# Two plain gate-and-up sets: 128 tokens stationary and 512 weight columns streaming, instead of 128 weight columns stationary and 256 tokens streaming

## The chip, the cores and the metric

One core of a Trainium2 chip. The time is device microseconds of one execution. TensorE multiplies; a matmul has a stationary operand of 128 x 128 (loaded by its own instruction, shown as PEld) and a moving operand whose columns stream past it; results gather in eight PSUM banks of 128 x 512 floats. VectorE, ScalarE and GpSimd work beside it, and SyncE issues most of the DMA transfers.

## The reference

One decoder layer on 512 tokens, model width 2048: a mixer (attention and gated delta rule, merged), and then the dense channel mixer, which is what the change touches:

```
h = rmsnorm(x, norm_ffn) * (1 + sc_f) + sh_f            # 512 x 2048
gate, up = split(h @ w_gate_up)                         # 2 x (512 x 5632)
x = x + gt_f * ((silu(gate) * up) @ w_down)             # 512 x 2048
return rmsnorm(x, final_norm)
```

## The kernel before

All matrix products are made in three parts: each operand is split into a high part (`hi`, a ScalarE cast) and a low part (`lo`, a VectorE subtraction), and hi*hi, hi*lo and lo*hi are summed in PSUM. Activations are held transposed, features on the partitions. The 512 tokens are two halves h of 256.

`h2T[h][q]` is the split, normalised input of the channel mixer for half h and two k blocks (k = 2q, 2q+1) of 128 features; `h2_gen(h)` (line 1743) makes it: sums of squares by eight small matmuls (`hss`, in `part_rstd`), the reciprocal root on VectorE and a diagonal (`diag`), one product with ones that spreads it over the partitions (`hbc`, in `spread`), and then for each q two VectorE operations, two of ScalarE and the split (`h2h`, `h2l`).

The 5632 gate and up columns are done in 12 sets. Set 0 and set 1 are plain, of 256 gate and 256 up columns each; the ten big sets, `big(1)` to `big(10)`, of 512 + 512 columns, use seven products in place of eight on operands that are combined ahead: `combine()` (line 1769) makes `comb[q]` in four groups, each of four sums and four splits.

Set 0 (`gu0`, built with the helper `fm_set`) is done for half 0 and then for half 1, because the second half of `h2T` is not ready at its start; both fetch all the weights. Set 1 (`gu_both(1)`) does both halves together. In both a block of 128 weight columns is stationary and 256 tokens stream; the result has columns on the partitions, four banks of (128 columns x 2 halves of 256 tokens). `gu_done` takes the silu of the two gate banks (ScalarE), multiplies by the up banks (VectorE) and writes the two tiles to `f_dram[s, h]`, which the down stage reads, features on the partitions.

A big set has tokens stationary and 512 weight columns streaming, so its results come out with tokens on the partitions. They are turned one big set later: `turned_a(b)` (line 1938), called in four of the units of each big set's second half (`if second and 1 <= k <= 4`), makes four 128 x 128 transposes on TensorE into a bank `aT`; ScalarE copies it to `f`, and GpSimd writes it to `f_dram`. It does nothing while the list `turning` is empty, as it is in `big(1)`.

The order of work. `Driver` runs a list of units. A unit is a weight load, a split, and a list of matmuls; loads run up to four units ahead and splits two; before a unit's matmuls its `pre` is called, and then the next split is put out, or only after the matmuls where the unit is `late`. Beside the units run side chains, generators such as `h2_gen` and `combine`. Each 12 matmuls (`GROUP`) the driver pumps: each chain makes one step, and a chain that yields n lets n pumps pass. `hold()` holds one pump back. Where a unit needs what a chain has not made, its `pre` steps the chain on at once: in `gu0`, `ahead` demands `h2n[h] >= min(2 * i + 4, 16)` k blocks before unit i; in `big`, `pre(i)` demands `xn[0] > i % 8 // 2` groups of `comb`. TensorE, SyncE and GpSimd keep the order in which the program puts instructions out; ScalarE's and VectorE's order is chosen when the kernel is built. Tiles of 128 x 512 come from 68 shared slots (`S`), and a new tile waits for a free one. All matmuls and DMA issues show line 155, so the profile is read by tile names.

## Time and profile before

| | us |
|---|---|
| runs, median of 3 | 2736.91 (2732.53 to 2739.21) |
| profiled execution, first to last instruction (the span) | 2731.7 |
| profiled execution, own time | not recorded apart from the span |
| TensorE busy | 2705.7 |
| set 0 (tile gu, from 1379.7) and set 1 | together to 1473.35 |
| first big set | 1473.35 to about 1549 |

The profile is of one execution. PE is TensorE's matmuls, PEld its weight loads, DVE VectorE, ACT ScalarE, POOL GpSimd. A row of a timeline has the start, the length, the engine, the line, the operation, output and inputs, and in brackets the idle time before it and who ended it. The chain that ended last is followed back from the last instruction; its rows have start, length, engine, tile and the number of instructions. Rows of stretches give busy time of PE, PEld, DVE, ACT and POOL with instruction counts, the granted clock of TensorE as a fraction, the share of the DMA engines and GB/s. Matmuls overlap, so their cost is the distance from start to start, not their length.

### The profile page before, as it was taken

The numbers are of one execution on the slowest core, as the hardware profiler recorded it, in microseconds if no ns is written. First come the engines' busy times: TensorE is split into PE (matmuls) and PEld (weight loads), VectorE is DVE, ScalarE is ACT, GpSimd is POOL, SyncE is SP. The second block draws the span as 40 slices with busy tenths as digits, with TensorE's granted clock in tenths as the row PEclk, the third lists the DMA queues.
The fourth block names the chain that finished last, engine by engine and source line by source line (L and its number), as shares of the span: only waits on it lengthen the run. The fifth ranks groups of instructions, "written<-read, shape, count | busy, mean of one in ns | idle before, by whom it ended". The sixth has DMA issues, their size and how long they took to land.

```text
span 2731.7 us, 41089 instructions
## 1 busy us (share of the span) xinstructions
PE 2705.7 (99%) x15304; PEld 2351.8 (86%) x15304; DVE 2098.3 (77%) x3361; ACT 1204.9 (44%) x1717; POOL 258.8 (9%) x361
## 2 busy tenths in 40 slices
PE   9999999999999999999999999999999999999998
PEld 7888788888888888889999888888888888998997
DVE  8784656677977886788787877778787777877877
ACT  3443432442344343234473444444444446446445
POOL 0000011102101000001000000000000103113113
PEclk9999999999999999999999999999999999999999
DMA  9896455646666978725854556665655668569565
GB/s 364 302 357 215 143 177 173 190 144 185 198 187 194 315 253 313 258 78 131 268 185 136 195 201 208 204 208 198 212 190 198 214 212 208 132 194 202 126 190 178
DMA packets 315489, 562.20 MB, mean 206 GB/s; under 512 B 40772, under 2 KB 120916, under 8 KB 315288
## 3 DMA queue, kind: packets, MB, share of 16 engines
q1 hardware_dynamic: 264776, 458.99, 51.6%
q0 software_dynamic: 31872, 74.76, 10.6%
q10 hardware_dynamic: 18640, 25.83, 2.7%
q8 instruction: 120, 1.97, 0.3%
q14 instruction: 81, 0.66, 0.1%
HBM read 476.62 MB, written 83.89 MB: 205 GB/s over the span
## 4 chain that ended last, share of the span: by engine, by line
PE 90%; DVE 4%; DMA 3%; issue 2%; ACT 1%; SPq 0%; DVEq 0%; ACTq 0%; POOL 0%
PE m L155 41%; PE gb L155 6%; PE v L155 4%; PE gu L155 3%; PE z L155 3%; PE ya L155 3%; PE k L155 3%; PE q L155 3%; PE yb L155 3%; PE dn L155 3%; PE s L155 3%; PE ckv L155 2%; PE cq L155 2%; PE wo L155 1%; PE qk L155 1%
## 5 line engine op out<-in xcount | busy, mean ns | idle before, releaser
L263 ACT CAST hi<-raw 128x1024 fp32r<-128x1024 f32 x249 | 258.8, 1041 | 538.9 <-DMA raw<-in_w_in_dram 164.9
L264 DVE TENSOR_TENSOR lo<-raw,hi 128x1024 fp32r<-128x1024 f32 x249 | 302.6, 1216 | 202.4 <-ACT hi L263 197.6
L1847 ACT CAST hi<-raws 128x512 fp32r<-128x512 f32 (+1 forms) x240 | 218.6, 911 | 328.0 <-PE m L155 269.2
L1848 DVE TENSOR_TENSOR lo<-raws,hi 128x512 fp32r<-128x512 f32 (+1 forms) x240 | 247.4, 1042 | 83.9 <-ACT hi L1847 83.6
L155 PE MATMUL m<-xh,lo 128*128 128x256 f32 x1088 | 308.4, 283 | 1.3 <-DVE lo L2023 1.3
L155 PE MATMUL m<-xh,hi 128*128 128x256 f32 x1088 | 308.1, 283 | 1.5 <-ACT hi L2022 1.5
L155 PE MATMUL m<-xl,hi 128*128 128x256 f32 x1088 | 307.9, 283 | 0.0
L449 DVE CUSTOM_DVE_ANT_0 rawm<-rawm,cbc 128x1024 f32<-128x1024 f32 x192 | 232.1, 1230 | 2.0 <-DMA rawm<-in_w_mod_dram 1.7
L155 PEld LDWEIGHTS m<-xh,lo 128*128 128x128 f32 x1088 | 208.8, 192 | 2.0 <-DVE lo L2023 1.9
L155 PEld LDWEIGHTS m<-xh,hi 128*128 128x128 f32 x1088 | 208.9, 192 | 1.7 <-ACT hi L2022 1.7
L155 PEld LDWEIGHTS m<-xl,hi 128*128 128x128 f32 x1088 | 208.9, 192 | 0.1
L155 PE MATMUL m<-hi,h2h 128*128 128x512 f32 x480 | 190.1, 396 | 0.0
L155 PE MATMUL m<-hi,h2l 128*128 128x512 f32 x480 | 187.2, 390 | 0.0
L155 PE MATMUL m<-lo,h2h 128*128 128x512 f32 x480 | 187.2, 390 | 0.0
L2022 ACT CAST hi<-sums 128x1024 fp32r<-128x1024 f32 x88 | 92.2, 1048 | 134.4 <-PE m L155 102.4
L2023 DVE TENSOR_TENSOR lo<-sums,hi 128x1024 fp32r<-128x1024 f32 x88 | 107.4, 1220 | 45.5 <-ACT hi L2022 45.4
L1847 ACT CAST hi<-sums 128x1024 fp32r<-128x1024 f32 x80 | 84.2, 1053 | 109.4 <-PE m L155 104.5
L1848 DVE TENSOR_TENSOR lo<-sums,hi 128x1024 fp32r<-128x1024 f32 x80 | 97.6, 1220 | 26.7 <-ACT hi L1847 26.1
L155 PEld LDWEIGHTS m<-hi,h2l 128*128 128x128 f32 x480 | 90.1, 188 | 19.0
L155 PEld LDWEIGHTS m<-hi,h2h 128*128 128x128 f32 x480 | 90.2, 188 | 18.5 <-DVE euvw L1865 0.7
L155 PEld LDWEIGHTS m<-lo,h2h 128*128 128x128 f32 x480 | 90.3, 188 | 17.5
L2022 ACT CAST hi<-raws 128x768 fp32r<-128x768 f32 x88 | 73.4, 835 | 66.8 <-PE m L155 48.1
(581 smaller groups left out, 7418.3 us busy)
## 6 DMA issues: line engine op xcount, KB each, us to landing
raws<-in_w_gate_up_dram SPq DMA_DIRECT2D x400, 256.0 KB, 3.6
rawm<-in_w_mod_dram SPq DMA_DIRECT2D x192, 512.0 KB, 5.4
raw<-in_w_in_dram SPq DMA_DIRECT2D x143, 512.0 KB, 4.6
raws<-in_w_down_dram SPq DMA_DIRECT2D x128, 256.0 KB, 3.9
s_dram<-raws POOLq DMA_DIRECT2D x80, 256.0 KB, 2.3
raws<-s_dram SPq DMA_DIRECT2D x80, 256.0 KB, 3.3
rawa<-in_w_in_dram SPq DMA_DIRECT2D x32, 512.0 KB, 4.6
raws<-in_w_o_dram SPq DMA_DIRECT2D x48, 256.0 KB, 3.1
```

Source lines behind the costliest of these rows:

```text
L155: return self.tc.keep_in_program_order(f(*args, **kwargs))
L263: nc.scalar.copy(hi[:], raw[:])
L264: (lo_eng or nc.vector).tensor_tensor(lo[:], raw[:], hi[:].bitcast(F32), ALU.subtract)
L449: r = nc.vector.tensor_tensor_reduce(raw, raw, c, 1.0, 0.0, ALU.mult, ALU.add, parts[:, k, half:half + 1])
L1847: nc.scalar.copy(hi[:], src)
L1848: nc.vector.tensor_tensor(lo[:], src, hi[:].bitcast(F32), ALU.subtract)
L2022: nc.scalar.copy(hi[:], src)
L2023: nc.vector.tensor_tensor(lo[:], src, hi[:].bitcast(F32), ALU.subtract)
```

## The change

Both plain sets are made by one function, `gu_tokens(s, hts)`: for each pair (half h, token block t of 128) it takes one bank, keeps 128 tokens of `h2T` stationary and streams the unit's 512 columns (256 gate, 256 up). Set 0 is still done half by half (two banks each), set 1 with four banks. `gu_read` reads a finished bank: silu of the left half, times the right half, into 256 columns of `first_tiles[h, t]`, set 0 on the left and set 1 on the right. The four tiles then stand in `turning`, and the first big set turns them with the calls that found nothing there before. `gu_done`, `gu_both`, the writes of its tiles and the pump held back at the end of set 0 are gone; the last unit of each half of set 0 is now `late`.

```diff
-    def gu_done(s, ps):
...
-                    nc.scalar.activation(f[h][:, fs], v, AF.Silu)
-                else:
-                    nc.vector.tensor_tensor(f[h][:, fs], f[h][:, fs], v, ALU.mult)
-                if j == 3:
-                    side(f_dram[s, h], f[h][:])
...
+    first_tiles = {}
+
+    def gu_read(s, ht, bank):
+
+        if s == 0:
+            first_tiles[ht] = S("g0")
+        o, g = first_tiles[ht][:, 256 * s:256 * s + 256], S("sl")
+        nc.scalar.activation(g[:, 0:256], bank[:, 0:256], AF.Silu)
+        nc.vector.tensor_tensor(o, g[:, 0:256], bank[:, 256:512], ALU.mult)
+
+    def gu_tokens(s, hts):
...
-                for j in range(4):
-                    for h in range(2):
-                        for n, (wi, xi) in enumerate(((0, 0), (0, 1), (1, 0))):
-                            mms.append(lambda kk=kk, k=k, j=j, h=h, n=n, wi=wi, xi=xi: mm(
-                                st["ps"][j][:, 256 * h:256 * h + 256], box["w"][wi][:, kk, tok(j)], half_k(h2T[h][k // 2], k)[xi],
...
+            def one(kk, h, t, n, xi, wi):
                 k = k0 + kk
+                mm(banks[h, t][:], half_k(h2T[h][k // 2], k)[xi][:, tok(t)], box["w"][wi][:, kk, :],
+                   start=k == 0 and n == 0, stop=k == KT - 1 and n == 2)
+                if k == KT - 1 and n == 2:
+                    gu_read(s, (h, t), banks.pop((h, t)))
+
+            mms = [lambda kk=kk, h=h, t=t, n=n, xi=xi, wi=wi: one(kk, h, t, n, xi, wi)
+                   for kk in range(2) for h, t in hts for n, (xi, wi) in enumerate(((0, 0), (0, 1), (1, 0)))]
 
             def post():
-                if k0 + 2 == KT:
+                if k0 + 2 == KT and s == 1:
                     for q in range(4):
                         h2T[1][q] = None
+                    turning.append((0, first_tiles))
...
+            return Unit(start, split, mms, pre, post, alone=s == 0, late=k0 + 2 == KT)
...
             for h in range(2):
-                half = fm_set("gu0", gu_loads(0), 512, KT, lambda k, h=h: half_k(h2T[h][k // 2], k), done if h else None, st=st,
-                              cols=slice(256 * h, 256 * h + 256), alone=True)
+                half = gu_tokens(0, [(h, t) for t in range(2)])
                 for i, u in enumerate(half):
                     def ahead(h=h, k=min(2 * i + 4, KT)):
                         while h2n[h] < k:
                             drv.step(h2c[h])
                     with_pre([u], ahead)
...
-        yield from with_pre(gu_both(1), lambda: xc.append(drv.add(combine())))
+        both = gu_tokens(1, [(h, t) for h in range(2) for t in range(2)])
+        yield from with_pre(both, lambda: xc.append(drv.add(combine())))
```

More of the change, by code (lines that the diff above doesn't have):

```diff
@@ L2138, in gu_loads @@
                                (lambda r: r[:, :, 256:512], wrows(w_gu, k0, nk, DFF + 256 * s, 256))]
-    def gu_done(s, ps):
-        f = {}
-        def done(j, h):
-            if h == 0:
-                return
-            for h in range(2):
-                fs, v = slice(256 * (j % 2), 256 * (j % 2) + 256), ps[j][:, 256 * h:256 * h + 256]
-                if j < 2:
-                    if j == 0:
-                        f[h] = S("sl")
-                    nc.scalar.activation(f[h][:, fs], v, AF.Silu)
-                else:
-                    nc.vector.tensor_tensor(f[h][:, fs], f[h][:, fs], v, ALU.mult)
-                if j == 3:
-                    side(f_dram[s, h], f[h][:])
-        return done
-    def gu_both(s):
-        st = {}
+    first_tiles = {}
[6 more added lines that the diff above has]
+    def gu_tokens(s, hts):
+        banks = {}
         def unit(k0):
@@ L2173, in pre @@
                 if k0 == 0:
-                    st["ps"] = [PS(f"gu{s}") for _ in range(4)]
-                    st["done"] = gu_done(s, st["ps"])
-            def after(j, h):
-                st["done"](j, h)
-            mms = []
-            for kk in range(2):
-                k = k0 + kk
-                for j in range(4):
-                    for h in range(2):
-                        for n, (wi, xi) in enumerate(((0, 0), (0, 1), (1, 0))):
-                            mms.append(lambda kk=kk, k=k, j=j, h=h, n=n, wi=wi, xi=xi: mm(
-                                st["ps"][j][:, 256 * h:256 * h + 256], box["w"][wi][:, kk, tok(j)], half_k(h2T[h][k // 2], k)[xi],
-                                start=k == 0 and h == 0 and n == 0, stop=k == KT - 1 and n == 2, skip_group_check=True))
-                        if k == KT - 1:
-                            mms[-1] = lambda m=mms[-1], j=j, h=h: (m(), after(j, h))
+                    for ht in hts:
+                        banks[ht] = PS(f"gu{s}")
+            def one(kk, h, t, n, xi, wi):
+                k = k0 + kk
+                mm(banks[h, t][:], half_k(h2T[h][k // 2], k)[xi][:, tok(t)], box["w"][wi][:, kk, :],
[4 more added lines that the diff above has]
+                   for kk in range(2) for h, t in hts for n, (xi, wi) in enumerate(((0, 0), (0, 1), (1, 0)))]
             def post():
-                if k0 + 2 == KT:
+                if k0 + 2 == KT and s == 1:
                     for q in range(4):
                         h2T[1][q] = None
-            return Unit(start, split, mms, pre, post, late=k0 + 2 == KT)
+                    turning.append((0, first_tiles))
+            return Unit(start, split, mms, pre, post, alone=s == 0, late=k0 + 2 == KT)
         return [unit(k0) for k0 in range(0, KT, 2)]
@@ L2218, in gu0 @@
         def gu0():
-            us, st = [], {}
-            def done(ps):
-                done_ = gu_done(0, ps)
-                for j in range(4):
-                    for h in range(2):
-                        done_(j, h)
+            us = []
             for h in range(2):
-                half = fm_set("gu0", gu_loads(0), 512, KT, lambda k, h=h: half_k(h2T[h][k // 2], k), done if h else None, st=st,
-                              cols=slice(256 * h, 256 * h + 256), alone=True)
+                half = gu_tokens(0, [(h, t) for t in range(2)])
                 for i, u in enumerate(half):
@@ L2234, in gu0 @@
                     with_pre([u], ahead)
-                us.append(half)
+                us += half
             def start():
@@ L2241, in start @@
                 start_h2(1)()
-            with_pre(us[0], start)
-            return us[0] + us[1]
+            with_pre(us, start)
+            return us
         def reload_a(k):
```

## The prediction

> **What bounds the kernel now.** I read the page first (busy time, then the chain that ended last), then stretches by stage, then the chain by pieces around the two plain sets, then the single engines there.

> ```profile
> span 2731.7 us, 41089 instructions
> PE 2705.7 (99%) x15304; PEld 2351.8 (86%) x15304; DVE 2098.3 (77%) x3361; ACT 1204.9 (44%) x1717; POOL 258.8 (9%) x361
> PE 90%; DVE 4%; DMA 3%; issue 2%; ACT 1%; SPq 0%; DVEq 0%; ACTq 0%; POOL 0%
> ```

> TensorE is busy for 99% of the span and carries 90% of the chain. The stretches below are set 0, set 1, the first big set and the second; columns are PE, PEld, DVE, ACT, POOL busy, granted clock, DMA share, GB/s.

> ```profile
> 1379.70:1427.00 47.30, 47.30 (x396) 47.25 (x395) 41.43 (x72) 36.59 (x57) 0.00 (x0) 1.00 0.60 190
> 1427.00:1473.30 46.30, 46.30 (x388) 46.30 (x387) 35.83 (x51) 19.08 (x32) 3.34 (x5) 1.00 0.44 120
> 1473.30:1546.40 73.10, 73.10 (x324) 60.49 (x323) 54.03 (x62) 30.00 (x33) 5.39 (x10) 1.00 0.56 183
> 1546.40:1619.50 73.10, 73.10 (x331) 60.52 (x331) 58.37 (x68) 32.21 (x41) 5.94 (x11) 1.00 0.61 206
> ```

> TensorE has no hole in any of them, so here a matmul saved is time saved, and a wait added is time added. VectorE is at 88% in set 0: the normalised input (h2) is still being made beside it. The chain by pieces (start, length, what, how many) gives the prices:

> ```profile
> 1379.88 7.20 PE gu L155 x60
> 1387.08 0.79 PE hss L155 x8
> 1387.87 8.74 PE gu L155 x72
> 1396.60 0.43 PE hbc L155 x2
> 1397.04 76.31 PE gu L155 x636
> 1473.35 127.90 PE m L155 x564
> 1601.24 0.44 PE aT L155 x4
> 1601.68 4.12 PE m L155 x18
> ```

> **The matmuls.** Removed: 768 matmuls of 256 columns (16 k, 4 column blocks, 2 halves, 3 products, 2 sets). They stand here as 60 + 72 + 636, at 76.31/636 = 0.120 us each: 92.2 us. Added: 384 of 512 columns (4 token blocks in place of 4 x 2). The same shape runs in the big sets at 127.90/564 = 0.2268 us: 87.1 us. Gain 5.1 us. Half the columns would be 0.1134 us, so each matmul carries some 13 ns beyond its columns, and 384 go.

> [...]

> **The turning.** In the first big set the slots for turning exist already but are empty; now each of four units does four transposes. In the next set such a unit takes 0.44 + 4.12 us against 18 x 0.2268 = 4.08 without: +0.48, four times: +1.9 us. Their four ScalarE copies and four GpSimd writes replace the four writes of before; as in every later big set they lie beside TensorE (no hole in the fourth stretch). If that cover went, TensorE would still not wait for the writes: only the down stage reads them.

> **The readers.** The same number of silus and products (8 each, 256 columns), moved: four now stand at the middle and end of set 0. With the first goes the table load:

> ```profile
> 1425.37 1.28 ACT L2152 ACT_TABLE_LOAD   x1
> 1426.66 1.21 ACT L2152 ACTIVATE sl<-gu 128x256 f32<-128x256 f32 x4
> ```

> It comes about 22 us earlier, at the end of the first half, when ScalarE has a cast behind it and a free stretch; I cost it at 0 and up to 1.3 us if it falls between the spread and h2. Weight loads and splits are unchanged in number: each half of set 0 still fetches all of its weights. That the last unit of each half is now filled late delays one load and one split by 2.7 us, of a lead of two units: 0.

> **The clock of the side chains.** This decides. Side chains advance one step for each 12 matmuls issued, and the matmuls are half as many. The chain that makes h2 of the second half starts with set 0: 3 steps to the sum of squares (hss), 6 more to the spread (hbc), then a pair of k every second step. The pieces show it: hss after 60 matmuls, hbc after 72 more, so hbc is issued at matmul 132 of 192, well inside the first half. After the change the first half has 96 matmuls. hss comes at matmul 60 of 96, and step 10 would fall at 132, in the second half. But the first unit of that half demands four k of h2, so the chain is forced there: hbc, then two pairs, directly in front of the matmuls that use them. TensorE is in program order; it must wait for the whole latency.

> ```profile
> 1398.70 0.87 DVE L1752 SCALAR_TENSOR_TENSOR h2f<-x,s_ffn,hbc 128x256 f32<-128x256 f32 x2
> 1399.49 1.22 DVE L264 TENSOR_TENSOR lo<-raw,hi 128x1024 fp32r<-128x1024 f32 x1
> 1400.92 0.69 DVE L240 TENSOR_TENSOR h2l<-h2f,h2h 128x512 fp32r<-128x512 f32 x1 [0.22 <-ACT h2h L239]
> 1401.53 0.87 DVE L1752 SCALAR_TENSOR_TENSOR h2f<-x,s_ffn,hbc 128x256 f32<-128x256 f32 x2
> ```
> ```profile
> 1399.33 0.91 ACT L1753 ACTIVATE h2f<-h2f,sh_ffn 128x256 f32<-128x256 f32 x2
> 1400.27 0.62 ACT L239 CAST h2h<-h2f 128x512 fp32r<-128x512 f32 x1
> ```

> That is the first pair of the second half, before the change. From its start to h2h 2.2 us, to h2l 2.9 us. The first two matmuls need h2h, the third h2l, so the two cover 0.45 of it; hbc's own result takes some 0.4 us more than its place on TensorE (0.43). Stall 2.9 - 0.45 + 0.4 = 2.9 us. Bounds: 2.2 us if nothing stands between; 4.9 us if the two products of the readers (0.41 each, the group below) and a split's 1.22 us stand ahead.

> ```profile
> L2154 DVE TENSOR_TENSOR sl<-sl,gu x8: 411/413/422, 1427.1 to 1473.8; 128x256 f32<-128x256 f32 x8
> ```

> ```profile
> 1387.90 0.16 DVE L417 TENSOR_SCALAR rs<-hss 128x2 f32<-128x2 f32 x1 [0.81 <-PE hss L155]
> 1395.59 0.48 DVE L1467 TENSOR_SCALAR diag<-kc,rs 128x128 f32<-128x128 f32 x2
> ```

> hbc needs diag, which came 8.2 us after hss. Now 36 matmuls lie between, 36 x 0.2268 = 8.2 us: even. I take +0.3 us, between 0 and 2. The pairs after it are emitted a unit ahead, and VectorE's round of a pair and a split is 1401.53 - 1398.70 = 2.83 us with the idle 0.22 in it; a unit of 12 matmuls is 2.72. As 0.22 is not work, 2.61 fits: +0.2 us, between 0 and 8 x 0.11 = 0.9.

> **The clock after the wait.** One wait on TensorE just ahead of this stage shows what follows a hole. The first fence is stretches, the second the waits, the third single matmuls.

> ```profile
> 1356.00:1358.00 2.00, 0.00 (x0) 0.03 (x1) 2.00 (x4) 0.63 (x1) 0.00 (x0) 1.00 0.35 131
> 1358.00:1360.00 2.00, 2.00 (x12) 2.00 (x13) 1.68 (x3) 0.00 (x0) 0.00 (x0) 0.66 0.67 223
> 1360.00:1362.00 2.00, 2.00 (x11) 2.00 (x11) 0.84 (x3) 0.09 (x1) 0.00 (x0) 0.50 0.69 219
> 1362.00:1364.00 2.00, 2.00 (x19) 2.00 (x18) 1.00 (x1) 0.96 (x1) 0.00 (x0) 0.99 0.82 268
> ```
> ```profile
> PE hss L155 <- DVE sq L1444: 2.2, 1, 2.2
> PE dn L155 <- DVE g L2038: 1.7, 1, 1.7
> ```
> ```profile
> 1359.92 0.41 PE L155 MATMUL wo<-a2h,hi 128*128 128x256 f32 x1
> 1360.13 0.41 PE L155 MATMUL wo<-a2l,hi 128*128 128x256 f32 x1
> ```

> After 2.2 us of waiting the granted clock was 0.66 and 0.50 in the next two stretches, and a matmul took 0.21 us in place of 0.12. At 0.50 for some 3.4 us, 1.4 to 1.7 us were lost. No other 2 us stretch before the last matmul is below 0.99, the one of the 1.7 us wait included. The new hole is about 2.9 us, nearer to the first; I take +1.4 us, bounds 0 and 1.7. [...]

> **The other side chain.** The combined operands of the big sets (comb) need 32 steps; set 1 gave 32, now 16. Two of four groups are then made inside the first big set, and forced at its units 4 and 6.

> ```profile
> 1441.58 0.68 DVE L240 TENSOR_TENSOR x6l<-x,x6h 128x512 fp32r<-128x512 f32 x1
> 1442.18 0.68 DVE L240 TENSOR_TENSOR x7l<-x,x7h 128x512 fp32r<-128x512 f32 x1
> 1443.38 0.68 DVE L1780 TENSOR_TENSOR x<-h2f,h2f 128x512 f32<-128x512 f32 x1
> 1463.96 0.68 DVE L1780 TENSOR_TENSOR x<-h2f,h2f 128x512 f32<-128x512 f32 x1
> 1554.81 1.22 DVE L1826 TENSOR_TENSOR sums<-raws,raws 128x1024 f32<-128x1024 f32 x1
> 1559.42 1.22 DVE L1826 TENSOR_TENSOR sums<-raws,raws 128x1024 f32<-128x1024 f32 x1
> ```

> A group is eight VectorE operations, 1442.18 - 1441.58 = 0.60 us apart: 4.8 us, so 9.6 us move. In the next set a unit of VectorE work, with one more such operation, takes 1559.42 - 1554.81 = 4.61 us, so 4.0 alone, against 24 x 0.2268 = 5.44 of TensorE: 1.4 us free in each unit, 8.6 over six. The third group ran at 1443.38, when step 17 of 32 was due about 9 us later, so VectorE's order lets ready work forward. I cost this at +0.1 us, bounds 0 and 9.6.

> **Sum.** -5.1 + 1.9 + 2.9 + 0.3 + 0.2 + 1.4 + 0.1 = +1.7 us on a span of 2731.7. The page has no time beside the span; the median of the runs is 2736.9, 5.2 above it (runs 2732.5 to 2739.2). On the median: 2738.6 us.

> **Rivals.** First, the stall without the fall of the clock: +0.3, 2737.2 us. [...] Second, no stall: the spread is ready and h2 arrives in time, -3.1, 2733.8 us. Against: hbc and its matmuls are adjacent in TensorE's order, and the pair takes 2.2 us at least. Third, slower: the two late groups are not brought forward. Then each is emitted just ahead of the unit that reads it, in ScalarE's and VectorE's queues behind casts that wait for TensorE; one group of 4.8 us at unit 4 and one at unit 6 come on top, +9.6 at most, 2748 us; it decides for slower once it costs over 6.5 us. For it: 8.6 us of free time for 9.6 of work, and four more tiles live in the shared slots; the fourth group before (1463.96) stood 20 us behind the third, so something held it. Fourth, it doesn't keep the matmul rate: the second half of set 0 goes at VectorE's 2.83 us a unit and each unit waits, +0.7 beside the forecast, 2739.3 us, which I count with the forecast.

> **How the numbers follow.** Chances: forecast 0.50, clock holds 0.27, no stall 0.08, late groups 0.15. What a measurement can tell from no change is 0.3%, 8.2 us. The forecast, the clock and the no-stall cases lie within it, but for a little; of the late groups two thirds reach beyond. So slower 0.10, same 0.88, faster 0.02 (the whole matmul gain is only 5.1). The range leaves out part of the no-stall case and the upper part of the late groups: with the 3 us that runs scatter, 2734 to 2745.

> **What would show it.** In the changed profile: gu matmuls 384, 0.227 us apart; aT 16 more, in the first big set; a wait of TensorE of 2 to 4 us for h2h or h2l of VectorE or ScalarE, right behind hbc, which stands at the middle of set 0 behind 96 gu matmuls; a granted clock below 1 behind it, or not; no TensorE wait in the first eight units of the first big set. Wrong would be: hbc ahead of the second half's matmuls by many units, a wait there of over 5 us, or waits for x5 to x7 in the first big set.

## The result, and the profile after

The changed kernel takes 2745.02 us (median of 5 runs, 2743.47 to 2748.71). The kernel before took 2734.86 us on the same chip in the same job. The ratio is 1.0041 with a 95% interval of 1.0030 to 1.0052, so the change makes the kernel slower by 0.4%, some 10 us. The forecast was +1.7 us and no measurable change.

The top of the page of the changed kernel:

```profile
span 2743.3 us, 40351 instructions
PE 2708.3 (99%) x14936; PEld 2334.7 (85%) x14936; DVE 2098.8 (77%) x3361; ACT 1207.5 (44%) x1721; POOL 259.3 (9%) x361
```

TensorE issues 368 matmuls fewer (384 out of the sets, 16 transposes in) and is 2.6 us longer busy; a busy TensorE is not a fast one. To see where the time went, the starts of the first matmul of four tiles cut the span into pieces that both kernels have: `m` of the wo stage (the mixer's output product), `gu` (set 0), `m` of the first big set, `dn` (down stage). The starts are read from the timeline of TensorE; the table has the distances in us.

| run | m (wo) to gu | gu to first big set | first big set to dn | dn to the end |
|---|---|---|---|---|
| before | 172.4 | 93.5 | 779.2 | 479.3 |
| before, run again | 172.6 | 93.5 | 779.6 | 481.4 |
| changed | 176.8 | 97.9 | 781.2 | 481.4 |
| changed, run again | 176.1 | 98.0 | 781.2 | 479.1 |

The last column scatters by 2 us in both. The change costs about 4 us **ahead of** set 0, where it edits nothing; 4.4 us in the two sets, where 0.3 less was forecast; and 1.9 us in the big sets, as forecast. The waits of TensorE in the changed kernel between 1200 and 1490 us (sum, number, longest) show the first two:

```profile
PE gu L155 <- ACT h2h L239: 4.4, 2, 4.3
PE hss L155 <- DVE sq L1444: 3.5, 1, 3.5
PE m L155 <- DVE lo L2023: 2.4, 1, 2.4
PE wo L155 <- DVE lo L264: 0.3, 1, 0.3
```

Before, hss waited 2.2 us and the others not at all.

**In set 0.** hbc starts at 1406.30 behind 96 gu matmuls, as forecast, and the first matmul of the second half waits 4.27 us. VectorE behind hbc:

```profile
1406.22 0.42 DVE L2148 TENSOR_TENSOR g<-sl,gu 128x256 f32<-128x256 f32 x1 [0.89 <-ACT sl L2147]
1407.58 1.23 DVE L264 TENSOR_TENSOR lo<-raw,hi 128x1024 fp32r<-128x1024 f32 x1 [0.93 <-DMA raw<-in_w_gate_up_dram]
1408.72 0.41 DVE L2148 TENSOR_TENSOR g<-sl,gu 128x256 f32<-128x256 f32 x1
1409.05 0.87 DVE L1752 SCALAR_TENSOR_TENSOR h2f<-x,s_ffn,hbc 128x256 f32<-128x256 f32 x2
```

A weight split and one reader's product stand between hbc and the first pair of h2: the upper bound of the forecast, not its middle. The granted clock (third number from the end) behind that wait, in stretches of 2 us:

```profile
1410.00:1412.00 2.00, 0.83 (x2) 0.61 (x3) 0.85 (x2) 1.08 (x3) 0.00 (x0) 0.53 0.78 254
1412.00:1414.00 2.00, 2.00 (x6) 1.60 (x6) 0.77 (x3) 1.52 (x3) 0.00 (x0) 0.50 0.00 0
1414.00:1416.00 2.00, 2.00 (x6) 1.54 (x5) 1.33 (x3) 0.91 (x2) 0.00 (x0) 0.50 0.00 0
1416.00:1418.00 2.00, 2.00 (x8) 1.59 (x7) 0.23 (x1) 1.31 (x2) 0.00 (x0) 0.76 0.00 0
```

Twelve matmuls are 0.427 us apart instead of 0.227, and the first 0.591, where it also waits for h2l: some 2.6 us. This size is not fixed. In three later runs of the same sets behind the same wait (4.27 us) the half rate ended sooner, as here, where the half begins at 1412.35 (the run without the transposes, under "The turning" below):

```profile
1412.00:1414.00 2.00, 1.65 (x4) 1.32 (x5) 1.48 (x3) 0.85 (x3) 0.00 (x0) 0.53 0.45 154
1414.00:1416.00 2.00, 2.00 (x7) 1.52 (x7) 0.96 (x2) 0.97 (x2) 0.00 (x0) 0.61 0.00 0
1416.00:1418.00 2.00, 2.00 (x10) 1.66 (x9) 0.51 (x2) 1.84 (x4) 0.00 (x0) 1.00 0.00 0
```

There the two sets took 96.6 to 96.8 us and not 97.9. Then, in the changed kernel, at the start of the fourth, sixth and eighth unit of the half the matmuls come as h2 allows:

```profile
1422.22 0.50 PE L155 MATMUL gu<-hi,h2h 128*128 128x512 f32 x1
1422.56 0.40 PE L155 MATMUL gu<-lo,h2h 128*128 128x512 f32 x1
1422.95 0.50 PE L155 MATMUL gu<-hi,h2l 128*128 128x512 f32 x1
1423.29 0.39 PE L155 MATMUL gu<-hi,h2h 128*128 128x512 f32 x1
```

Distances of 0.34, 0.39 and 0.34 us instead of 0.227 cost 0.4 us, three times (at 1422, 1428 and 1434), and 0.7 us at 1403 with the wait of 0.16. TensorE's list of waits shows almost none of this: the 0.11 to 0.16 us that each distance is too long are less than a matmul's own 0.39 to 0.50. The weight loads beside them stand 0.31 us for h2h and 0.43 us for h2l (1422.22 and 1422.95).

**Ahead of set 0.** On TensorE, VectorE, ScalarE and SyncE both programs have the same instructions in the same order up to there. On GpSimd they don't. The GpSimd queue before, and then after, from 1306 and from 1305 us to set 1:

```profile
1428.50 1.08 POOL L155 DMA_DIRECT2D f_dram<-sl  x2 [122.70 <-DVE sl L2154]
1429.57 1.18 POOL L155 DMA_DIRECT2D g_dram<-gt_ffn  x1
```
```profile
1305.05 1.19 POOL L155 DMA_DIRECT2D g_dram<-gt_ffn  x1
1463.71 0.56 POOL L155 DMA_DIRECT2D s_dram<-raws  x1 [157.47 <-DVE raws L1826]
```

`g_dram<-gt_ffn` is the line behind the plain sets in `ffn`: `side(g_dram.rearrange("(k p) -> p k", p=P), gt_ffn[:])`, 2048 floats, of which the 16 of a partition go 128 floats apart. It is ready long before. What held it back was the queue: in front of it stood the two f_dram writes of set 0, which waited 122.7 us for their data. The change took these writes away, and the write of g went out 124.5 us earlier, into the wo stage. There the stretches of the changed kernel (last columns: granted clock, DMA share, GB/s) are

```profile
1308.00:1310.00 2.00, 2.00 (x19) 2.00 (x18) 1.30 (x2) 0.84 (x2) 0.00 (x0) 1.00 0.99 337
1310.00:1312.00 2.00, 2.00 (x19) 2.00 (x19) 0.00 (x0) 0.01 (x1) 0.00 (x0) 1.00 1.67 160
1312.00:1314.00 2.00, 2.00 (x19) 2.00 (x18) 0.00 (x0) 1.04 (x1) 0.00 (x0) 1.00 0.81 53
1314.00:1316.00 2.00, 2.00 (x19) 2.00 (x18) 0.00 (x0) 0.00 (x0) 0.00 (x0) 1.00 0.71 65
1316.00:1318.00 2.00, 1.30 (x11) 1.10 (x10) 0.36 (x1) 0.38 (x1) 0.00 (x0) 1.00 0.22 46
```

The DMA share is 1.67 and then 0.81 while 337 GB/s become 160 and 53. In the list of DMA issues the write takes 13.3 us from issue to landing:

```profile
g_dram<-gt_ffn POOLq DMA_DIRECT2D x1, 8.0 KB, 13.3
```

The wo loads land later beside it: between 1290 and 1330 us the median is 7.0 us and the longest 11.2, and 5.7 and 8.3 in the kernel before. VectorE's wait for the same load, before and after:

```profile
1312.56 0.69 DVE L2014 TENSOR_TENSOR sums<-raws 128x512 f32<-128x512 f32 x1 [2.06 <-DMA raws<-in_w_o_dram]
```
```profile
1317.64 0.69 DVE L2014 TENSOR_TENSOR sums<-raws 128x512 f32<-128x512 f32 x1 [8.34 <-DMA raws<-in_w_o_dram]
```

Six us later on VectorE make the 2.4 us wait of TensorE in m, and VectorE, being late, makes sq late for hss. The same write stood in set 1 of the kernel before and did the same to the DMA engines there:

```profile
1434.00:1438.00 4.00, 4.00 (x35) 4.00 (x35) 3.94 (x6) 1.55 (x3) 0.00 (x0) 1.00 0.42 36
1438.00:1442.00 4.00, 4.00 (x36) 4.00 (x35) 3.75 (x6) 3.13 (x5) 0.00 (x0) 1.00 0.59 18
```

There it cost TensorE nothing: it is at 4.00 of 4.00 us. That its loads ran far enough ahead is the likely reason; it is not shown. In the changed kernel the 8 KB took 13.3 us to land, beside 256 KB transfers whose medians were 5.5 to 7.0 us (1295 to 1330 us). How much of it the layout of the write costs is not shown: no run wrote the same 8 KB in long rows.

That was read from traces. The runs had to show it.

### The profile page after: what moved, and what is told of

It reads as the page before. It is cut to its first block, busy times and chain, and to the rows that moved or that the text cites. A ratio compares the mean times of both kernels' runs of the same rounds, so it can differ in the third digit from the quotient of the medians.

```text
span 2743.3 us, 40351 instructions
## 1 busy us (share of the span) xinstructions
PE 2708.3 (99%) x14936; PEld 2334.7 (85%) x14936; DVE 2098.8 (77%) x3361; ACT 1207.5 (44%) x1721; POOL 259.3 (9%) x361
## 4 chain that ended last, share of the span: by engine, by line
PE 45%; DVE 3%; issue 1%; DMA 1%; ACT 1%; POOL 0%; DVEq 0%; SPq 0%; ACTq 0%; POOLq 0%
PE m L155 37%; PE gu L155 3%; PE dn L155 3%; PE wo L155 1%; PE aT L155 1%; DMA raws<-in_w_down_dram 1%; DVE sums L2014 0%; DVE lo L2023 0%; DVE xl L240 0%; DVE lo L264 0%; DMA x<-x_dram 0%; DVE sq L1444 0%; DMA raw<-in_w_o_dram 0%; ACT hi L2022 0%; PE dnt L155 0%
## 5 line engine op out<-in xcount | busy, mean ns | idle before, releaser
L263 ACT CAST hi<-raw 128x1024 fp32r<-128x1024 f32 x249 | 258.8, 1041 | 540.1 <-DMA raw<-in_w_in_dram 156.4
L264 DVE TENSOR_TENSOR lo<-raw,hi 128x1024 fp32r<-128x1024 f32 x249 | 302.6, 1217 | 208.4 <-ACT hi L263 200.1
L155 PE MATMUL m<-xh,lo 128*128 128x256 f32 x1088 | 308.3, 283 | 2.7 <-DVE lo L2023 2.7
L155 PE MATMUL m<-xh,hi 128*128 128x256 f32 x1088 | 308.0, 283 | 1.1 <-ACT hi L2022 1.1
L155 PE MATMUL m<-xl,hi 128*128 128x256 f32 x1088 | 307.9, 283 | 0.0
L155 PEld LDWEIGHTS m<-xh,lo 128*128 128x128 f32 x1088 | 208.9, 192 | 3.5 <-DVE lo L2023 3.5
L155 PEld LDWEIGHTS m<-xh,hi 128*128 128x128 f32 x1088 | 208.9, 192 | 1.4 <-ACT hi L2022 1.3
L155 PEld LDWEIGHTS m<-xl,hi 128*128 128x128 f32 x1088 | 208.9, 192 | 0.1
L155 PE MATMUL m<-hi,h2h 128*128 128x512 f32 x480 | 190.4, 397 | 0.4 <-DVE euvw L1865 0.4
L155 PE MATMUL m<-hi,h2l 128*128 128x512 f32 x480 | 187.2, 390 | 0.0
L155 PE MATMUL m<-lo,h2h 128*128 128x512 f32 x480 | 187.1, 390 | 0.0
L2022 ACT CAST hi<-sums 128x1024 fp32r<-128x1024 f32 x88 | 92.2, 1048 | 132.8 <-PE m L155 94.0
L155 PEld LDWEIGHTS m<-hi,h2l 128*128 128x128 f32 x480 | 90.1, 188 | 18.9
L155 PEld LDWEIGHTS m<-hi,h2h 128*128 128x128 f32 x480 | 90.2, 188 | 18.3 <-DVE euvw L1865 0.8
L155 PEld LDWEIGHTS m<-lo,h2h 128*128 128x128 f32 x480 | 90.3, 188 | 17.6
```

The source lines that it names most:

```text
L155: return self.tc.keep_in_program_order(f(*args, **kwargs))
L263: nc.scalar.copy(hi[:], raw[:])
L264: (lo_eng or nc.vector).tensor_tensor(lo[:], raw[:], hi[:].bitcast(F32), ALU.subtract)
L2022: nc.scalar.copy(hi[:], src)
```

## The experiments

**The pump.** The first question was whether the loss in the sets comes from the side chains' clock, as predicted. Two kernels change it alone, and the changed kernel and the kernel before run again beside them. In the changed kernel each gu matmul counts two for the pump:

```diff
-            return Unit(start, split, mms, pre, post, alone=s == 0, late=k0 + 2 == KT)
+            return Unit(start, split, mms, pre, post, weight=2, alone=s == 0, late=k0 + 2 == KT)
```

> The changed kernel, but each of its 384 wide matmuls counts twice for the pump, so the side chains (h2 of the second half, comb) step at the rate per microsecond that they had before the change. Theory 1 (the slower side chains cost the time: the forced spread and the slow clock behind it): hbc stands well ahead of the second half again, no TensorE wait there, the granted clock stays at 1.00 through set 0, gu matmuls take 384 x 0.227 = 87 us without a hole; against the kernel before -5.1 + 1.9 = -3.2 us, ratio about 0.999. Theory 2 (a good part of the +10 us lies outside the two plain sets, in the stages ahead and the down stage, because of the change): it stays 4 to 5 us above that, ratio 1.000 to 1.001. Theory 3 (the token-major form itself is dear, its reads and the turning): it stays near 1.003.

In the kernel before, each counts a half:

```diff
-            return Unit(start, split, mms, pre, post, late=k0 + 2 == KT)
+            return Unit(start, split, mms, pre, post, weight=0.5, late=k0 + 2 == KT)
...
+                    u.weight = 0.5
```

> The kernel before with nothing changed but that each matmul of the two plain sets counts half for the pump, the rate of side chains per microsecond that the change brought. Theory 1: hbc directly ahead of the second half of set 0, a TensorE wait of 3 to 5 us there, then 1.4 to 2.7 us of slow clock: +5 to +7 us, ratio 1.002 to 1.0026. Theory 3: no difference from the kernel before, below 1 us.

> The changed kernel once more, as it is. By theory 1 its profile shows the same wait of about 4.3 us behind hbc and the slow clock after it, two plain sets of 97 to 98 us, and the stages ahead of set 0 and behind the big sets as in the kernel before within 2 us either way (what differed there was scatter of the transfers). By theory 2 they are again 3 us and 2 us longer than in the kernel before.

> The kernel before once more, for the scatter of its stages: by theory 1 the stages ahead of set 0 differ from the first profile (1379.7 us) by up to some 3 us, the down stage by up to 2 us; by theory 2 both lie within 1 us of it.

| run | median us | ratio to before, 95% | m to gu | gu to first big set | to dn |
|---|---|---|---|---|---|
| changed, weight 2 | 2741.84 | 1.0033 (1.0020 to 1.0046) | 176.7 | 94.4 | 781.8 |
| before, weight 0.5 | 2741.38 | 1.0029 (1.0020 to 1.0038) | 172.2 | 100.1 | 781.1 |
| changed again | 2743.69 | 1.0037 (1.0025 to 1.0049) | 176.1 | 98.0 | 781.2 |
| before again | 2737.06 (one run) | | 172.6 | 93.5 | 779.6 |

Halving the pump alone makes the kernel before 6.6 us longer in the two sets and nowhere else by more than 2: the mechanism is real. Its waits there, all on the h2 chain, with 3.4 us of half rate behind the first:

```profile
PE gu L155 <- ACT h2h L239: 2.2, 1, 2.2
PE gu L155 <- DVE h2l L240: 1.3, 5, 0.3
```

Giving the pump back to the changed kernel wins 3.5 us in the sets (97.9 to 94.4), but the run stays 0.3% slower, which the theory didn't allow. (Theory 3 named this ratio; for the sets the order by halves below decides against it, since there the same form takes 4.6 us less than the kernel before.) Two things remained. In the sets, hbc now comes early and waits itself, and the fourth unit of the second half waits for its h2:

```profile
PE gu L155 <- ACT h2h L239: 2.6, 1, 2.6
PE hbc L155 <- DVE diag L1467: 1.5, 1, 1.5
```

And the 4 us ahead of gu were still there, with the pump untouched in that stage. They are in both runs of the changed kernel and in this one, and in none of the kernel before. That led to the GpSimd queue.

**The write of g, moved alone.** In the kernel before, the write is put ahead of the f_dram writes, where the change puts it in effect:

```diff
                 start_h2(1)()
+                side(g_dram.rearrange("(k p) -> p k", p=P), gt_ffn[:])
...
-        side(g_dram.rearrange("(k p) -> p k", p=P), gt_ffn[:])
```

> The kernel before with one instruction moved on the GpSimd queue: the write g_dram<-gt_ffn comes directly behind the eight x reloads and ahead of the first two f_dram writes, where the change puts it in effect. Theory A: m to gu grows from 172.4 to 176 to 177 us, with a wait in m for lo or a longer wait of hss, gu to m2 stays at 93.5; so about 4 us more than the kernel before, ratio 1.0015. Theory B: nothing changes, ratio 1.000.

2740.24 us, 1.0019 (1.0010 to 1.0028). m to gu 176.4, gu to the first big set 93.5. The waits of TensorE from 1200 to 1490 us and VectorE's wait for the load:

```profile
PE hss L155 <- DVE sq L1444: 3.3, 1, 3.3
PE m L155 <- DVE lo L2023: 1.1, 1, 1.1
```
```profile
1316.29 0.69 DVE L2014 TENSOR_TENSOR sums<-raws 128x512 f32<-128x512 f32 x1 [7.06 <-DMA raws<-in_w_o_dram]
```

One instruction moved on one queue gives both waits and 4 us ahead of gu, with nothing else of the change. The waits are 2.1 us more than before; the half rate behind hss lasts 6.8 us in place of 3.4, which is worth another 1.7 by estimate (half of 3.4). Theory A holds. (The median is 6.7 us above the kernel before in that job; what is more than the 4 lies in this profile behind gu, in stages that scatter by some 2 us.)

**The write of g, held back.** In the changed kernel, the write is put out in the first big set, behind five s_dram writes:

```diff
-        side(g_dram.rearrange("(k p) -> p k", p=P), gt_ffn[:])
...
+                if (s, i) == (1, 2):
+                    with_pre([u], lambda: side(g_dram.rearrange("(k p) -> p k", p=P), gt_ffn[:]))
```

> The changed kernel with one instruction moved on the GpSimd queue: the 8 KB write of gt_ffn in single elements (g_dram<-gt_ffn) comes behind five of the first big set's s_dram writes and no longer directly behind the eight x reloads. Theory A (this write, which the change let go some 125 us earlier, takes the DMA engines from the wo weights): from the first matmul of m to the first of gu 172.2 to 172.6 us as in the runs of the kernel before (176.1 to 176.8 with the change); the wait in m for the split lo gone and the wait of hss back at 2.2 to 2.5 us; gu to m2 unchanged at 97.9; so about 4 us less than the changed kernel, some 2740.3 us, ratio to the kernel before 1.0022. Theory B (the time ahead of gu is lost to something else, such as the places of the tiles): 176 us remain there, ratio 1.004.

2749.38 us, 1.0056 (1.0043 to 1.0068): a miss, slower than the change itself. The piece ahead of gu did recover (173.9, hss back at 2.3 us, no wait in m), but from the first big set to dn it took 789.4 us and not 781.2. The write, now issued at 1495.58, held back a weight load of that set, and VectorE stood for it:

```profile
1511.44 1.23 DVE L1826 TENSOR_TENSOR sums<-raws,raws 128x1024 f32<-128x1024 f32 x1 [9.21 <-DMA raws<-in_w_gate_up_dram]
```
```profile
PE m L155 <- DVE x5l L240: 6.1, 1, 6.1
```

So the write isn't dear at one place: it cost some 4 us in the wo stage (176.4 in place of 172.4) and 8.2 in the first big set (789.4 in place of 781.2), and in both a load beside it was needed soon. What I expected of the run took its cost to be zero in the new place, the same step that had failed in the prediction.

**The write of g, where it was.** GpSimd is made to wait for it by data: the write goes from a copy of gt_ffn that takes the last made h2f of the second half times zero.

```diff
+        def write_g(q):
+            t = C("gt_late", [P, KT])
+            nc.vector.scalar_tensor_tensor(t[:], h2f[1][q][:, 0:KT], 0.0, gt_ffn[:], op0=ALU.mult, op1=ALU.add)
+            side(g_dram.rearrange("(k p) -> p k", p=P), t[:])
...
-        yield from with_pre(both, lambda: xc.append(drv.add(combine())))
-        side(g_dram.rearrange("(k p) -> p k", p=P), gt_ffn[:])
+        with_pre(both, lambda: xc.append(drv.add(combine())))
+        yield from with_pre(both, lambda: write_g(7))
```

> The changed kernel with the write g_dram sent from a copy of gt_ffn that VectorE makes at the start of set 1 (a copy of 128 x 16 that takes h2f of the second half times zero, so that it can't be made sooner): the write leaves at some 1430 us, where the kernel before has it (1429.57), and not at 1305 as with the change nor at 1496 as in the run that held it back to the first big set. Theory (the write is to be hidden only where the loads in flight are not needed soon): m to gu 172 to 174 us, gu to m2 96.8 to 97.9, no wait of 6 us in the first big set, m2 to dn 781.2; 2743.7 - 4 = 2739.7 us, ratio 1.002 (1.001 to 1.003). Rival (the write costs its 4 us wherever it lies): a wait of some us within set 1 or at the start of the first big set, ratio 1.0035 or more.

2742.89 us, 1.0029 (1.0019 to 1.0040). The write leaves at 1429.16, as it did before the change, and m to gu is 172.2 us:

```profile
1429.16 1.18 POOL L155 DMA_DIRECT2D g_dram<-gt_late  x1 [123.69 <-DVE gt_late L2416]
```
```profile
PE gu L155 <- ACT h2h L239: 4.4, 2, 4.3
PE hss L155 <- DVE sq L1444: 2.2, 1, 2.2
```

Ahead of gu the loss is gone, in the sets (96.6) it stays, 1.3 us smaller with the shorter half rate (3.4 us), and no new wait of several us stands between 1200 and 1490 us. The whole time fell by less than the 4 us expected, to 7.2 us above the kernel before; of this profile's excess, 1.9 us lie between the first big set and dn (783.1), where two waits for euvw (1.12 and 0.25 us) stand that come and go between runs of one kernel. The time is within its interval of what the theory gave.

**The clock.** In the changed kernel 18 matmuls without use are put between hbc and the second half's first matmul, so that TensorE doesn't idle; the half can't start earlier by it. They read a tile that is there and write a bank that nobody reads.

```diff
+                if h:
+                    ahead0 = half[0].pre
+
+                    def padded():
+                        ahead0()
+                        pad, t = PS("pad"), h2T[0][0][0]
+                        for _ in range(18):
+                            mm(pad[:], t[:, 0:P], t[:], start=True, stop=True)
+                    half[0].pre = padded
```

> The changed kernel with 18 matmuls without use (128 x 512, 0.227 us each, 4.1 us together) between hbc of the second half and that half's first gu matmul. They fill the 4.27 us wait; h2h is not earlier by them, so the first gu matmul of the half starts where it did. Theory A (TensorE's idling is what brings the granted clock down to 0.5): the clock stays at 1.00, the 13 matmuls behind the wait are 0.227 apart and no longer 0.427, gu to m2 falls from 97.9 to 95.3 and the time by 2.6 us, ratio to the kernel before 1.0028. Theory B (the clock falls for another reason, such as the kind of work that follows): 97.9 or a little more, ratio 1.0037 or above.

2743.04 us, 1.0035 (1.0022 to 1.0047), beside 1.0037 and 1.0041 for the changed kernel: on the whole time it can't be told. In the trace it can: gu to the first big set is 95.5 (97.9 and 98.0 without), a wait of 0.16 in place of 4.27 us, and the stretches around the half's start (1414.82) read

```profile
1412.00:1414.00 2.00, 2.00 (x10) 1.68 (x9) 1.56 (x4) 0.80 (x2) 0.00 (x0) 1.00 0.19 28
1414.00:1416.00 2.00, 1.84 (x7) 0.91 (x7) 1.21 (x3) 0.82 (x3) 0.00 (x0) 1.00 0.69 236
1416.00:1418.00 2.00, 2.00 (x11) 1.60 (x10) 0.76 (x2) 1.44 (x3) 0.00 (x0) 1.00 0.00 0
```

The clock stays at 1.00 where it read 0.50 without them, so its fall there is the idling's. On top of the wait it is worth 2.4 to 2.5 us against the two profiles of the changed kernel, and 1.1 to 1.3 us against the three with the shorter half rate (96.6 to 96.8). (In this profile m to gu is 178.6, some 2 us more than in the others.)

**The turning.** In the changed kernel the four tiles of the two sets are written to f_dram as they lie, without the 16 transposes and the four copies:

```diff
-                    turning.append((0, first_tiles))
+                    for h in range(2):
+                        for t in range(2):
+                            side(f_dram[t, h], first_tiles[h, t][:])
```

> The changed kernel without the turning of the two first sets' results in the first big set: their four tiles are written to f_dram as they lie, so 16 transposes and four ScalarE copies are left out and the down projection reads these rows of f in the wrong layout (its products are other numbers at the same cost). Theory (turning costs 4 units x 0.48 us): m2 to dn 781.2 - 1.9 = 779.3 us, as in the kernel before (779.2 and 779.6), the rest as with the change. Rival (the turning lies beside other work, and m2 to dn is 2 us longer through waits): 781 us still.

In this one execution (2740.94 us), from the first big set to dn 779.3 us, with m to gu at 177.2 and gu to the first big set at 96.6: the turning is 1.9 us. The first big set alone takes 76.2 us (76.2 and 77.0 in the kernel before), and 78.0 with the turning, in which TensorE has no wait.

**The order by halves.** If the loss in the sets is that the second half begins too soon, it goes when both sets of the first half run ahead of it. Set 1's weights are then loaded and split twice. The write of g is held back to the first big set, as in the run above; the weight of 1.5 keeps the chains' rate between the two kernels'.

```diff
-            return Unit(start, split, mms, pre, post, alone=s == 0, late=k0 + 2 == KT)
+            return Unit(start, split, mms, pre, post, weight=1.5, alone=True, late=k0 + 2 == KT)
...
-                us += half
+                second = gu_tokens(1, [(h, t) for t in range(2)])
+                us += half + (with_pre(second, lambda: xc.append(drv.add(combine()))) if h else second)
...
```

> The changed kernel in another order: set 0 and set 1 of the first half of the tokens, then set 0 and set 1 of the second half, so that 192 wide matmuls and no longer 96 run ahead of the second half's first one; set 1's weights are loaded and split a second time for it (8 units more), each matmul of these sets counts 1.5 to the pump, and g_dram<-gt_ffn is held back as in the run with that alone. Theory A (the loss is the stall behind hbc with its slow clock, the second half's chain, and the early write): m to gu 172.4, gu to m2 88 to 89 (384 x 0.2268 = 87.1 and the hss and hbc matmuls), m2 to dn 781.2; so 2731.5 us, 0.999 of the kernel before (0.9985 to 0.9995). Rival: the eight splits more (1.22 us on VectorE each) hold the second half's chain back, gu to m2 stays over 92 and the ratio is 1.000 to 1.001.

2748.34 us, 1.0049 (1.0036 to 1.0062), and yet gu to the first big set is 88.9, as theory A had it, and m to gu 170.8, 1.6 us below it (the clock did not fall behind hss). From the first big set to dn it took 794.8. The held write, issued at 1483.43, looked like the cause again: one wait of 9.9 us.

```profile
PE m L155 <- DVE x7l L240: 9.9, 1, 9.9
```

With the write sent from the copy at the fifth unit of set 0's second half (`write_g(5)`) instead:

> The order by halves (set 0 and 1 of the first half, then of the second) with the write g_dram sent from such a copy at the fifth unit of set 0's second half, some 1430 us. The run of this order with the write in the first big set had m to gu 170.8, gu to m2 88.9 and then one wait of 9.9 us for x7l at 1503. Theory (that wait is the write's): it is gone, m2 to dn is 781.2, and the time falls by 13.6 us from 2748.3 to some 2734 less the noise of the rest, 2731 to 2735 us, ratio 0.9985 to 1.000. Rival (the order by halves itself leaves comb late, since the second half's chain ends nearer to the first big set): the wait for x7l stays, 2740 us or more.

2739.75 us, 1.0016 (1.0007 to 1.0025). m to gu 172.2. The two sets:

```profile
1380.60:1469.50 88.90, 88.90 (x397) 73.18 (x396) 71.32 (x109) 57.07 (x83) 1.74 (x2) 1.00 0.65 193
```

No wait, full clock, 4.6 us less than the kernel before. But to dn it takes 786.1 us, with a wait of 2.95 us for x7l in place of 9.9. Part of the 9.9 was the write's, part is the order's: the rival is half right. The combined operands come too late in the first big set, which takes 82.8 us and not 78.0. So the last run starts their generator six units earlier:

```diff
+                    if (h, i) == (1, 2):
+                        with_pre([u], lambda: xc.append(drv.add(combine())))
...
-                us += half + (with_pre(second, lambda: xc.append(drv.add(combine()))) if h else second)
+                us += half + second
```

> The order by halves with the write sent at some 1426 us, and the generator that makes comb (x3, x6, x7, x5) started at the third unit of set 0's second half and no longer at set 1's second half, six units of 2.72 us earlier, where VectorE has gaps of 0.7 to 2.6 us between the splits. Theory (in the run of that order the 2.95 us wait for x7l at 1498.6, and the slow clock behind it, came from comb's last group being made 29 us into the first big set, one group too late): no wait for x7l, m to gu 172.2, gu to m2 88.9, m2 to dn 781.2 and no longer 786.1; 4.9 us less than 2739.75, 2734.9 against 2735.7 for the kernel before in that job, ratio 0.9997 (0.9985 to 1.001). Rival (VectorE is full in the first big set whatever the order): another wait of 2 us or more stays in the first big set, m2 to dn 784 or more, ratio 1.001 or above.

2738.29 us, 1.0010 (1.0002 to 1.0019): the wait for x7l is gone, and another stands at 1473, for a bank that VectorE reads late:

```profile
PE m L155 <- DVE g L2148: 2.3, 1, 2.3
```
```profile
1470.00:1474.00 4.00, 1.69 (x8) 1.09 (x7) 2.68 (x5) 0.97 (x3) 0.00 (x0) 1.00 0.26 99
```

To dn it is 786.5 us; 3.5 of the 5.3 us beyond 781.2 lie in the first big set (81.5 us), most of the rest in waits for euvw in a later one. The rival's signs, another wait of over 2 us and more than 784, are there; that VectorE is full whatever the order is not shown by one order. This version is 0.1% behind the kernel before and, by the ratios of two jobs, 0.3% ahead of the change. No version here beats the kernel before.

## Why the prediction was wrong

By its own steps, with what was measured for each:

| step | forecast us | measured us | shown by |
|---|---|---|---|
| 768 matmuls to 384 | -5.1 | -4.6 | order by halves: 88.9 in place of 93.5, no wait in it |
| turning | +1.9 | +1.9 | 781.2 with, 779.3 without |
| stall behind hbc | +2.9 (2.2 to 4.9) | +4.3 | wait of 4.27 |
| clock after it | +1.4 (0 to 1.7) | +2.4 to 2.6; +1.1 to 1.3 in three other profiles | dummy matmuls: 95.5 in place of 97.9, or of 96.6 to 96.8 |
| diag late | +0.3 (0 to 2) | 0 | diag made at 1400.63, hbc at 1406.30 without a wait |
| VectorE's round | +0.2 (0 to 0.9) | +1.9 | distances at 1403, 1422, 1428, 1434 |
| combined operands late | +0.1 | 0 | no wait in the first big set |
| writes replaced, other queues | 0 | +4 | the write of g moved alone: 176.4 in place of 172.4 |

With 2.5 for the clock, as in the two profiles of the changed kernel, they sum to +10.0 us, against +10.2 (first job) and +9.4 (second) measured; with 1.2 it would be +8.7, so that the sum comes out this near is in part luck.

**The step that failed** is "Their four ScalarE copies and four GpSimd writes replace the four writes of before". It priced the writes that moved and not the instruction behind them on GpSimd. The four writes of before had a second part: two of them stood at the head of an in-order queue until set 0 was done and kept the write of g behind them out of the wo stage. Taking a waiting instruction off a queue lets out what is behind it, and this was the largest term that the forecast missed; with 4 us more the forecast would have been +5.7. No rival had it. The trace of before showed all that was needed: the 122.7 us wait on the f_dram writes, `g_dram<-gt_ffn` right behind it at 1429.57, and DMA engines half busy at 36 and 18 GB/s from 1434 to 1442.

**The second step that failed is the size of what h2 costs.** The stall was in the right place and too small. hbc came behind 96 matmuls, and the wait was for h2h, as "the clock of the side chains" said; the run of the kernel before with half the pump shows that mechanism alone. But the split and one product that were the upper bound stood in front of the pair. The split waited for a cast that waited for TensorE's last matmuls of the half (1407.58, behind the cast of 1406.50), so it could not run earlier, and VectorE's order kept the pair behind it. That the half's last unit is `late` was priced at 0; no run tried it.

**The clock** fell, as the forecast and not the first rival had it. Its size came from one row, 3.4 us of half rate in the wo stage. In the changed kernel the half rate lasted 6.8 us, from 1410.12, and 5.8 of them lay on the half's matmuls; in three other profiles the same wait of 4.27 us gave 3.4 us, and +1.4 would have been about right. So the term could not be had from one row: in these profiles the length came in steps of 3.4 us (below), and the length of the wait did not settle how many.

**VectorE's round** was called +0.2 since 2.61 us of work fit into units of 2.72. They fit on average, not at the first matmuls of every second unit, which wait for h2h and h2l; the fourth rival named this and gave it 0.7.

**The late combined operands**, the rival given 0.15, did not show in the changed kernel: no TensorE wait between 1480 and 1600. They did show in the order by halves, at 2.95 us.

**The matmul saving was real.** The rows of this kernel (0.120 us for 256 columns, 0.2268 for 512) priced it well for these matmuls, each of which has a new stationary operand: 4.6 of 5.1 us were found again.

## What to carry to other kernels

When a change removes an instruction from an in-order queue, look at what stood behind it: a wait at the head of the queue is also a gate, and work that was held there by accident will start as soon as its own data allow. List the instructions behind each removed or moved one, with the time at which each could run, and ask what they meet there. A small write can be dear through the loads beside it: the 8 KB write of g cost some 4 us in the wo stage and 8.2 in the first big set. Look for a place where no load beside it is needed soon, and make data or a queue keep it there.

Where side chains advance by a count of matmuls, fewer and larger matmuls slow the chains; rescale the count with the change. Halving the pump alone cost 6.6 us here. In a kernel that is bound by one engine at 99%, saving 5 us on it is kept only if the producers beside it finish as much earlier.

## What the runs showed of the hardware

The length of the wait alone did not decide whether the clock fell. Waits of 1.54 and 2.59 us (the doubled pump), 2.31 and 2.95 us (the order by halves), with matmuls of 512 columns behind them, left it at 1.00:

```profile
1498.00:1500.00 2.00, 1.39 (x6) 1.05 (x6) 2.00 (x3) 0.55 (x2) 0.00 (x0) 1.00 0.87 260
```

That is the stretch behind the 2.95 us. A wait of 2.16 us in set 0 (the kernel before with half the pump) brought it to 0.50, and so did 4.27, 6.15 and 9.94 us. Ahead of hss, where eight matmuls of one column (0.8 to 1.3 us) stand behind the wait, 1.84 and 2.02 us (the last run, and the order by halves with the write held back) left it at 1.00, and 2.13 to 3.83 us brought it to 0.50 in the twelve other profiles. The two without the fall have 170.6 and 170.8 us from m to gu, the others with the write out of the way 172.2 and more, so it is worth some 1.5 us there. What decides whether it falls, and what part the one-column matmuls have in that, no run tried.

The DMA share of the changed kernel read 1.67 at 160 GB/s and then 0.81 at 53 GB/s (1310 to 1314 us) while the 8 KB write of g was under way, and 1.70 at 147 and 0.65 at 72 GB/s in the kernel before with the write moved. It took 12.3 to 13.8 us to land in the wo stage, in six runs with it there, and the waits for a load of another queue beside it were 7.06 and 8.34 us in the two traces shown, instead of 2.06.
